# Layer 0 of a diffusion backbone: its six modulation units at every second step instead of at six steps in a row

## The chip, the core and the metric

The kernel runs on one core of one Trainium2 chip. The metric is the device time of one execution in microseconds (us). TensorE is written PE in the profile, VectorE DVE, ScalarE ACT, GpSimd POOL and SyncE SP.

## The reference, cut to what matters

Four layers work on 512 latent tokens x and 256 context tokens, each 1024 wide. Layers 0 and 3 are latent attention (MLA), layer 1 is windowed attention, layer 2 a long convolution. Ahead of each layer a vector of 3072 numbers is computed from the conditioning vector (cond @ w_mod: shift, scale and gate): shift and scale modulate the layer's input, and the gate scales its output.

```
for layer in range(DEPTH):
    mx = cond_x @ w_mod[layer] + b_mod[layer]
    mc = cond_c @ w_mod[layer] + b_mod[layer]
    shift_x, scale_x, gate_x = jnp.split(mx[:, None, :], 3, axis=-1)
    ...
    hx = rmsnorm(x, g_pre[layer]) * (1.0 + scale_x) + shift_x
    ...
    x = x + gate_x * rmsnorm(yx, g_post[layer])
def mla_mixer(hx, hc, w_in, g_q, w_q, g_kv, w_kv, w_out, with_ctx_out):
    cq_x, ckv_x, kr_x, gate_x = jnp.split(hx @ w_in, split_at, axis=-1)
    q_x = queries(cq_x, True)                  # rmsnorm(cq) @ w_q, rotary
    k_x, v_x = keys_values(ckv_x, kr_x, True)  # rmsnorm(ckv) @ w_kv
    ...
    y_x = (o_x.reshape(b, n, A_WIDTH) * jax.nn.silu(gate_x)) @ w_out
```

w_mod is 4 x 1024 x 3072 float32, that is 12 MB for a layer. It is read once and each number is used for two rows only, so its product costs TensorE little and the transfer queues much.

## The kernel before

The 768 tokens are six tiles of 128. Every matmul of weights with tokens is done as three products of a split pair (high and low part, lines 577 to 579 for a token tile, line 588 for a gate). The program is written tile by tile in Python, and a scheduler with its own timeline puts each engine's instructions in their final order; so moving a call moves instructions on all engines, later ones too.

**Two streams of weights.** Both take 512 KB chunks (4 KB in each of 128 partitions) through staging slots in the arena F, and all of their transfers are issued by SP from one queue in program order (line 211). A `Stream` issues the transfer of a chunk as soon as a slot is free and fewer than `cap_d` chunks wait. `W` carries the layers' own weights: a chunk is split into its high and low parts by ACT (line 230) and by DVE or POOL (line 233), and then its slot is free. `M` carries w_mod: a chunk is used as it comes by four matmuls of 256 columns (line 442), and its slot is free after them.

**A modulation unit** is 512 of the 3072 columns, four chunks, 16 matmuls L442 (the trace keeps two records for each, 32 in all). Units of kind "ab" (shift and scale of the next layer) then copy the result to the arena (ACT, line 455), turn it by four transposes (line 459) and add the bias (DVE). Units of kind "g" (the gate of this layer) copy it (line 480) and load a bias row (line 481). The copy of a unit lies in the arena F too, among the staging slots. `self.fill()` writes the next unit into the program. Layer 0 writes six: four "ab" of layer 1, and two "g" of layer 0; they are called unit 1 to unit 6 below.

**The steps of `layer_A` before attention** are 6 key tiles (`ps[:, 0:320]`, 24 matmuls of 320 columns each), 6 cq tiles (24 matmuls of 512 columns each), and 8 gates (24 matmuls of 512 and 24 of 256 columns each, weights ("gate", c) of 512 KB). The norm of a tile (`normed`) turns it by transposes too (line 721), and the rotary key is turned in line 761. Before the change a unit comes ahead of the key tiles 3, 4 and 5 and of the cq tiles 0, 1 and 2. From key tile 3 on, `M` may hold two chunks (`MC = 2`); after the gates one.

**The output of a layer** (`w_out_phase`): six token tiles, 48 matmuls L606 each, in two alternating pairs of PSUM banks (pb_69, pb_70). A tile is multiplied by the gate vector `g` and added to x by DVE (`post`, lines 566 and 567), which frees its banks for the next tile but one. `gates_out` (lines 483 to 499) makes `g` from the two "g" units: four matmuls (line 494) and four DVE products (line 495).

Layer 1's own modulation calls are in code that the change does not touch; they take chunks through the same streams.

Of the kernel before, what the change touches and what calls it, by code (L numbers as in the profile page):

```python
# [29 lines left out]
SU = 2  # L30
WX = {25: (3, 2), 27: (3, 2), 29: (3, 3)}
UKS = (3, 4)
UQ = 0
UC = 0
MC = 2
CH = ((0, 384),)
LS = 2
# [98 lines left out]
class Ring:  # L136
# [6 lines left out]
    def next(self):  # L143
        self.i += 1
        return self.blocks[self.i % len(self.blocks)]
# [125 lines left out]
class Kern:  # L271
# [430 lines left out]
    def layer_A(self, L, j, h, ctx_out, last):  # L702
# [9 lines left out]
        def normed(ps, n, dst, t):  # L712

            ssq = self.col()
            nc.scalar.activation(self.trash[:, 0:n], ps, AF.Square, accum_out=ssq)
            self.rstd(ssq, n)
            cn = self.fs(n)
            nc.vector.tensor_scalar(cn.ap, ps, ssq, None, op0=ALU.mult)
            pt = self.a()
            for k in range(n // P):  # L720
                nc.tensor.transpose(pt[:, P * k:P * k + P], cn.ap[:, P * k:P * k + P], self.ident)
            cn.free()
            self.split_ps(dst[:, 0, :, P * t:P * t + P], dst[:, 1, :, P * t:P * t + P],
                          pt[:, 0:n].rearrange("p (k n) -> p k n", n=P))

        UK = UKS[0 if ctx_out else 1]
        units = sum(f[:2] in (("ab", L + 1), ("g", L)) for f in self.fillers)

        wide = Banks(self.halves())
        ckv = self.rl(2 * 2 * T)  # L730
# [6 lines left out]
        self.W.pump(4, 3)  # L737
        wk = lambda k: (ws[k // 2][1][0][:, k % 2], ws[k // 2][1][1][:, k % 2])
        for t in order:
            if t == UK:  # L740
                self.M.cap_d = self.M.look_d = MC
            if units and t >= UK:
                self.fill()
                units -= 1
            ps = wide.next()
            self.mm_tok(ps[:, 0:320], h, t, wk, 320)
            normed(ps[:, 0:256], 256, ckvv, t)
            ks = small.next()
            kv4 = ks.v(2, 2, 64)
            if t < 4:  # L750
                kf = self.ropes.next()
                self.rope_ps(kf.v(1, 64), ps[:, 256:320].rearrange("p (a b) -> p a b", a=1), t, 1)
                src = kf.ap[:, 0:64]
            else:
                kf = None
                src = ps[:, 256:320]
            nc.scalar.activation(kv4[:, 0], src[:, None, :].to_broadcast([P, 2, 64]), AF.Copy)
            nc.vector.tensor_tensor(kv4[:, 1], src[:, None, :].to_broadcast([P, 2, 64]), kv4[:, 0].bitcast(F32), op=ALU.subtract)
            pt = self.a()
            for i in range(2):  # L760
                nc.tensor.transpose(pt[:, P * i:P * i + P], ks.ap[:, P * i:P * i + P].bitcast(F32), self.ident)
            nc.vector.tensor_copy(krv[:, :, P * t:P * t + P], pt[:, 0:256].rearrange("p (a b) -> p a b", a=2))
# [4 lines left out]
        cqv = cq.v(2, 4, TQ)  # L767
        ws = [self.W.take(("cq", k)) for k in range(0, KD, 2)]
        for t in (order if ctx_out else qt):
            if units and t >= UQ:  # L770
                self.fill()
                units -= 1
            ps = wide.next()
            self.mm_tok(ps, h, t, wk, 512)
            normed(ps, 512, cqv, t)
# [2 lines left out]

        spans = [(0, NX), (NX, NC)] if ctx_out else [(0, NX)]
        for c in range(8):  # L780
            if units and c >= UC:
                self.fill()
                units -= 1
            blk, (wh, wl) = self.W.take(("gate", c))
            outs = [self.a()[:, 0:n] for _, n in spans]
            self.mm_ch(outs, lambda part, k, i: self.h_at(h, part, k, *spans[i]), lambda k: (wh[:, k], wl[:, k]))
            blk.free()
            for (t0, n), o in zip(spans, outs):
                self.gate2(ogv[:, c, t0:t0 + n], o)
# [157 lines left out]
        units = [(hd, t) for hd in range(8) for t in qt]  # L947
# [891 lines left out]
```

## Time and profile before

| | us |
|---|---|
| median of 3 runs | 1942.29 (1940.02 to 1943.27) |
| the profiled execution, its own time | 1944.16 |
| its span in the trace | 1942.3 |
| TensorE busy in the span | 1817.6 |
| mean granted TensorE clock | 0.984 of full speed |

The span runs from the first to the last recorded instruction; 1.9 us of the profiled execution's time lie outside it. TensorE is busy for 94% of the span, so the time is that of TensorE's work and of the places where it waits.

### The profile page before, as it was taken

Reading aid. Unit: us, or ns where it says so; the run is one execution under the profiler, and the core shown is the slowest. Engines: PE = TensorE matmul, PEld = TensorE weight load, DVE = VectorE, ACT = ScalarE, POOL = GpSimd, SP = SyncE. Lnnn points to the kernel's source line nnn. Section 1 sums busy time; section 2 is a strip of 40 time slices with the busy share of each in tenths; the row PEclk is TensorE's granted clock in tenths of the full one; section 3 lists DMA queues with packets and bytes.
Section 4 is the critical chain, followed back from the end, with each engine's and each line's share of the span. In section 5 each row is a group of like instructions: output and inputs, shape, how many; then the busy total and the mean of one; then the engine's idle time right before and its main releaser. Section 6 shows DMA issues by size and latency. Waiting matters only on the chain. (4 is left out here: it accounts for less than half of the span.)

```text
span 1942.3 us, 30290 instructions
## 1 busy us (share of the span) xinstructions
PE 1817.6 (94%) x11628; PEld 1575.6 (81%) x11628; DVE 1172.8 (60%) x2365; ACT 813.3 (42%) x1688; POOL 520.7 (27%) x523
## 2 busy tenths in 40 slices
PE   5889899999999899999989999999989899999998
PEld 3567588999988888888858789999988687889986
DVE  6684234787755367777675456555665554477663
ACT  3463132554544255565654522222222353354451
POOL 5562000000223321222231344444443221000120
PEclk9899899999999999999999999999999899999999
DMA  7867521001133212222363622222222334410121
GB/s 217 251 178 228 163 77 33 22 23 45 44 109 109 66 54 78 77 74 68 100 216 108 201 80 69 76 76 77 77 66 65 106 123 142 108 34 23 44 66 65
DMA packets 186356, 186.31 MB, mean 96 GB/s; under 512 B 16600, under 2 KB 164952, under 8 KB 186212
## 3 DMA queue, kind: packets, MB, share of 16 engines
q1 hardware_dynamic: 186212, 184.39, 30.8%
q8 instruction: 91, 1.49, 0.3%
q14 instruction: 53, 0.43, 0.1%
HBM read 160.24 MB, written 24.12 MB: 95 GB/s over the span
## 5 line engine op out<-in xcount | busy, mean ns | idle before, releaser
L588 PE MATMUL pb<-arena_r 128*128 128x512 f32 (+1 forms) x1488 | 278.9, 341 | 1.6 <-ACT arena_r L555 1.2
L341 ACT ACTIVATE arena_r<-pa 128x384 fp32r<-128x384 f32 (+2 forms) x382 | 175.4, 479 | 205.4 <-PE pa L909 68.0
L588 PEld LDWEIGHTS pb<-arena_r 128*128 128x128 f32 x1488 | 228.4, 189 | 33.1 <-ACT arena_r L555 1.7
L342 DVE TENSOR_TENSOR arena_r<-pa,arena_r 128x384 fp32r<-128x384 f32 (+2 forms) x382 | 199.7, 537 | 86.7 <-ACT arena_r L341 84.7
L588 PE MATMUL pa<-arena_r,swing_R 128*128 128x512 f32 (+1 forms) x816 | 165.7, 355 | 0.6 <-DVE arena_r L342 0.4
L588 PEld LDWEIGHTS pa<-arena_r,swing_R 128*128 128x128 f32 x816 | 132.2, 188 | 21.9 <-DVE arena_r L342 0.6
L884 PE MATMUL pb<-arena_r 128*128 128x384 f32 (+1 forms) x720 | 141.4, 336 | 3.0 <-ACT arena_r L341 1.8
L606 PE MATMUL pb<-arena_r 128*128 128x512 f32 x552 | 135.5, 398 | 2.6 <-ACT arena_r L230 2.6
L233 POOL TENSOR_TENSOR swing_R<-arena_f,swing_R 128x1024 fp32r<-128x1024 f32 (+1 forms) x33 | 77.2, 2344 | 194.1 <-ACT swing_R L230 144.2
L606 PEld LDWEIGHTS pb<-arena_r 128*128 128x128 f32 x552 | 103.4, 190 | 26.0 <-ACT arena_r L230 2.9
L884 PEld LDWEIGHTS pb<-arena_r 128*128 128x128 f32 x720 | 118.9, 188 | 5.1 <-ACT arena_r L341 2.5
L679 POOL TENSOR_TENSOR arena_f<-arena_f 128x128 f32<-128x128 f32 (+1 forms) x44 | 21.0, 478 | 356.6 <-DVE small L892 180.2
L233 POOL TENSOR_TENSOR arena_r<-swing_F,arena_r 128x1024 fp32r<-128x1024 f32 x36 | 87.6, 2434 | 86.2 <-ACT arena_r L230 81.1
L358 POOL TENSOR_SCALAR small<-small 128x1 f32<-128x1 f32 x68 | 17.2, 253 | 345.7 <-ACT trash L564 145.8
L923 PE MATMUL pa<-arena_r 128*128 128x256 f32 x624 | 91.5, 286 | 2.1 <-DVE arena_r L342 2.1
L923 PEld LDWEIGHTS pa<-arena_r 128*128 128x128 f32 x624 | 81.8, 189 | 4.8 <-ACT arena_r L341 2.5
L1079 PE MATMUL pa<-swing_R,arena_r 128*128 128x256 f32 x576 | 78.8, 285 | 5.0 <-DVE arena_f L348 3.8
L442 PE MATMUL pa<-arena_f,cst 128*32 128x256 f32 x744 | 57.4, 410 | 24.8 <-DMA arena_f<-in_w_mod_dram 24.8
L888 DVE TENSOR_REDUCE small<-pb 128x1 f32<-128x768 f32 (+1 forms) x80 | 67.6, 847 | 21.5 <-PE pb L884 20.7
L230 ACT ACTIVATE arena_r<-swing_F 128x1024 fp32r<-128x1024 f32 x39 | 41.4, 1063 | 91.9 <-PE pb L588 55.9
L891 ACT ACTIVATE arena_f<-pb,small 128x768 f32<-128x768 f32 (+1 forms) x80 | 65.2, 817 | 32.8 <-DVE small L889 26.4
L1079 PEld LDWEIGHTS pa<-swing_R,arena_r 128*128 128x128 f32 x576 | 71.4, 189 | 7.3 <-DVE arena_f L348 5.2
(268 smaller groups left out, 4216.6 us busy)
## 6 DMA issues: line engine op xcount, KB each, us to landing
arena_f<-in_w_mod_dram SPq DMA_DIRECT2D x93, 512.0 KB
swing_F<-in_c_w_in_dram SPq DMA_DIRECT2D x31, 512.0 KB
kd<-arena_f SPq DMA_DIRECT2D x48, 256.0 KB
arena_f<-in_a_w_in_dram SPq DMA_DIRECT2D x24, 512.0 KB
arena_f<-kd SPq DMA_DIRECT2D x16, 768.0 KB
arena_f<-in_b_w_in_dram SPq DMA_DIRECT2D x20, 512.0 KB
x<-arena_f SPq DMA_DIRECT2D x18, 512.0 KB
arena_f<-in_a_w_out_dram SPq DMA_DIRECT2D x16, 512.0 KB
```

The costliest lines, as they stand in the source:

```text
L230: nc.scalar.activation(hi, view, AF.Copy)
L233: eng.tensor_tensor(lo, view, hi.bitcast(F32), op=ALU.subtract)
L341: self.nc.scalar.activation(hi, src, AF.Copy)
L342: self.nc.vector.tensor_tensor(lo, src, hi.bitcast(F32), op=ALU.subtract)
L442: nc.tensor.matmul(ps[32 * j:32 * j + 32, n0:n0 + 256], self.cst[:, 4 * kh + j, :], w[:, j, :], start=(kh == 0), stop=(kh == 1), skip_grou ...
L588: nc.tensor.matmul(out, l, rhs(part, k, i), start=(k == 0 and q == 0), stop=(k == kt - 1 and q == 2))
L606: nc.tensor.matmul(ys[:, 512 * hf:512 * hf + 512], ov[:, a, k - ks.start], wt[:, 0, 512 * hf:512 * hf + 512], start=(k == 0 and q == 0), s ...
L884: nc.tensor.matmul(S[:, 512 * b:512 * b + w], l, r[:, k0 + w * b:k0 + w * b + w], start=(q == 0), stop=(q == 4))
L888: nc.vector.tensor_reduce(mx, Sv, axis=AX.XY, op=ALU.max)
L891: nc.scalar.activation(pr.v(nb, w), Sv, AF.Exp, bias=mx, scale=sc, accum_out=sm)
L923: nc.tensor.matmul(o[:, 0:256], vv[:, a_, kt % 3, P * hh:P * hh + P], ptv[i // nh][:, b_, i % nh], start=(i == 0 and q == 0), stop=(i == n ...
L1079: nc.tensor.matmul(ps[:, 0:256], self.h_at(h, part, k, P * t, P), w, start=(k == 0 and i == 0), stop=(k == KD - 1 and i == 2))
```

## The change

A generator `modulate()` counts the steps: key tiles are steps 0 to 5, cq tiles 6 to 11, gates 12 to 19. In layer 0 it writes a unit at step 3 and at every second step from there: ahead of the key tiles 3 and 5, the cq tiles 1, 3 and 5, and of the second gate. In layer 3 the pitch is one and the first step is 4, as before.

```
-UQ = 0
-UC = 0
+UP = (2, 1)
...
-        UK = UKS[0 if ctx_out else 1]
         units = sum(f[:2] in (("ab", L + 1), ("g", L)) for f in self.fillers)
+
+        def modulate():
+
+            first, pitch = (UKS[0], UP[0]) if ctx_out else (UKS[1], UP[1])
+            for i in range(99):
+                if i == first:
+                    self.M.cap_d = self.M.look_d = MC
+                if i >= first and (i - first) // pitch < units and (i - first) % pitch == 0:
+                    self.fill()
+                yield
+
+        mods = modulate()
...
         for t in order:
-            if t == UK:
-                self.M.cap_d = self.M.look_d = MC
-            if units and t >= UK:
-                self.fill()
-                units -= 1
+            next(mods)
...
         for t in (order if ctx_out else qt):
-            if units and t >= UQ:
-                self.fill()
-                units -= 1
+            next(mods)
...
         for c in range(8):
-            if units and c >= UC:
-                self.fill()
-                units -= 1
+            next(mods)
```

The number of instructions of every kind on every engine stays what it was; their order changes. The lines after the constants move up by one (L442 becomes L441).

**First place: TensorE at unit 4.** Before, this is what stands in TensorE's order from the last chunk of unit 3 to the second cq tile. `pa_66<-arena_f,cst` is a chunk's matmuls, `pa_67<-ident,arena_f` the unit's transposes, `pb` a cq tile.

```order
L578 MATMUL pb_70<-swing_R,arena_r 128x512
L442 MATMUL pa_66<-arena_f,cst 32x256 x4
L579 MATMUL pb_70<-swing_R,arena_r 128x512
L577 MATMUL pb_70<-swing_R,arena_r 128x512
L578 MATMUL pb_70<-swing_R,arena_r 128x512
L579 MATMUL pb_70<-swing_R,arena_r 128x512
L459 MATMUL pa_67<-ident,arena_f 128x128 x4
L442 MATMUL pa_66<-arena_f,cst 32x256 x16
L721 MATMUL pa_68<-ident,arena_f 128x128 x4
L577 MATMUL pb_69<-arena_r 128x512
L578 MATMUL pb_69<-arena_r 128x512
```

After the change unit 4 begins between the third and the fourth cq tile, with one chunk alone (the second L441 row here; the first is unit 3's last chunk).

```order
L441 MATMUL pa_65<-arena_f,cst 32x256 x4
L577 MATMUL pb_69<-swing_R,arena_r 128x512
L578 MATMUL pb_69<-swing_R,arena_r 128x512
L576 MATMUL pb_69<-swing_R,arena_r 128x512
L577 MATMUL pb_69<-swing_R,arena_r 128x512
L578 MATMUL pb_69<-swing_R,arena_r 128x512
L576 MATMUL pb_69<-swing_R,arena_r 128x512
L577 MATMUL pb_69<-swing_R,arena_r 128x512
L578 MATMUL pb_69<-swing_R,arena_r 128x512
L458 MATMUL pa_66<-ident,arena_f 128x128 x4
L441 MATMUL pa_65<-arena_f,cst 32x256 x4
L720 MATMUL pa_67<-ident,arena_f 128x128 x4
```

The other three chunks of unit 4 follow one at a time. Its last one stands among the last matmuls of the fourth cq tile, and its transposes and the first chunk of unit 5 (the second L441 row here) behind them, ahead of the sixth cq tile:

```order
L576 MATMUL pb_69<-swing_R,arena_r 128x512
L441 MATMUL pa_65<-arena_f,cst 32x256 x4
L577 MATMUL pb_69<-swing_R,arena_r 128x512
L578 MATMUL pb_69<-swing_R,arena_r 128x512
L458 MATMUL pa_66<-ident,arena_f 128x128 x4
L720 MATMUL pa_67<-ident,arena_f 128x128 x4
L441 MATMUL pa_65<-arena_f,cst 32x256 x4
L720 MATMUL pa_68<-ident,arena_f 128x128 x4
```

Between unit 3's last chunk and unit 4's first there stood four matmuls of the cq tile, and now there are eight; unit 5's first chunk has two matmuls and eight transposes ahead of it. The sixteen L442 matmuls in a row are gone.

**Second place: SP's queue in layer 0**, from unit 3's last chunks on. `in_w_mod_dram` is a chunk of modulation, `in_a_w_in_dram 128x8x128` a gate's weights, `in_a_w_q_dram` the weights of the queries. Before:

```order
L211 DMA arena_f<-in_a_w_in_dram 128x8x128 x2
L211 DMA arena_f<-in_w_mod_dram 128x4x256 x2
L211 DMA arena_f<-in_a_w_in_dram 128x8x128 x2
L211 DMA arena_f<-in_w_mod_dram 128x4x256 x7
L481 DMA arena_f<-in_b_mod_dram 1x512
L211 DMA arena_f<-in_w_mod_dram 128x4x256 x2
L481 DMA arena_f<-in_b_mod_dram 1x512
L211 DMA arena_f<-in_a_w_in_dram 128x8x128 x3
L209 DMA arena_f<-in_a_w_q_dram 128x4x64 x4
```

After:

```order
L210 DMA arena_f<-in_a_w_in_dram 128x8x128 x3
L210 DMA arena_f<-in_w_mod_dram 128x4x256 x12
L210 DMA arena_f<-in_a_w_in_dram 128x8x128 x2
L210 DMA arena_f<-in_w_mod_dram 128x4x256
L480 DMA arena_f<-in_b_mod_dram 1x512
L208 DMA arena_f<-in_a_w_q_dram 128x4x64 x3
L210 DMA arena_f<-in_w_mod_dram 128x4x256
L208 DMA arena_f<-in_a_w_q_dram 128x4x64
L210 DMA arena_f<-in_w_mod_dram 128x4x256
L210 DMA arena_f<-in_a_w_in_dram 128x8x128 x3
```

Ahead of the first row here SP issues thirteen of the 24 chunks before, and nine after. Before, four gates come close together, with two chunks between them; after, three gates come first, then twelve chunks without a gate, and the last three chunks are strung out among gates and query weights.

**Third place: TensorE at layer 1's output**, where the change moves instructions though its own lines do not run there. Before, this is the first token tile (pb_70) and the beginning of the second (pb_69), with the last four matmuls of attention (L1188); every chunk of the two "g" units (L442) stands ahead of these rows:

```order
L1188 MATMUL pa_67<-arena_r 128x256 x2
L606 MATMUL pb_70<-swing_R,arena_r 128x512 x14
L606 MATMUL pb_70<-arena_r 128x512 x2
L1188 MATMUL pa_67<-arena_r 128x256 x2
L606 MATMUL pb_70<-arena_r 128x512 x16
L494 MATMUL pa_66<-arena_f,sel 128x512
L606 MATMUL pb_69<-swing_R,arena_r 128x512 x4
L606 MATMUL pb_70<-arena_r 128x512 x4
L494 MATMUL pa_65<-arena_f,sel 128x512
L606 MATMUL pb_70<-arena_r 128x512 x8
L494 MATMUL pa_67<-arena_f,sel 128x512
L606 MATMUL pb_69<-swing_R,arena_r 128x512 x14
```

After, from the end of the first token tile to the first matmuls of the third, which uses pb_70 again (L605 was L606, L493 was L494):

```order
L441 MATMUL pa_65<-arena_f,cst 32x256 x12
L605 MATMUL pb_70<-arena_r 128x512 x8
L493 MATMUL pa_68<-arena_f,sel 128x512
L493 MATMUL pa_66<-arena_f,sel 128x512
L605 MATMUL pb_69<-swing_R,arena_r 128x512 x14
L441 MATMUL pa_65<-arena_f,cst 32x256 x4
L605 MATMUL pb_69<-arena_r 128x512 x30
L493 MATMUL pa_65<-arena_f,sel 128x512
L493 MATMUL pa_67<-arena_f,sel 128x512
L605 MATMUL pb_70<-swing_R,arena_r 128x512 x18
```

Five chunks, 20 matmuls L441, have gone from the end of attention into the first two tiles of the output (one of the five, a group of four, stands a few rows ahead of these). The last two matmuls of `gates_out` now stand right ahead of the third tile; before, they stood within the first. On DVE the four products L494 (L495 before), then L565 and L566 of the first tile follow each other in this order. Further up, in layer 1's attention, each of the first six units stands in three groups of chunks, where it stood in two.

## Rows read from the trace of the kernel before

**Rows 1.** The page: busy time of the engines in the span.

```profile
PE 1817.6 (94%) x11628; PEld 1575.6 (81%) x11628; DVE 1172.8 (60%) x2365; ACT 813.3 (42%) x1688; POOL 520.7 (27%) x523
```

**Rows 2.** Windows of 10 us: busy PE, PEld, DVE, ACT, POOL; clock; DMA share; GB/s.

```profile
190.00:200.00 10.00, 9.27 (x68) 6.25 (x67) 3.12 (x7) 3.32 (x8) 1.49 (x4) 1.00 0.87 261
200.00:210.00 10.00, 2.30 (x22) 1.07 (x24) 1.72 (x4) 1.11 (x2) 0.00 (x0) 0.67 0.76 212
210.00:220.00 10.00, 10.00 (x66) 6.54 (x62) 1.97 (x5) 1.20 (x2) 0.00 (x0) 0.81 0.50 160
220.00:230.00 10.00, 8.59 (x61) 5.50 (x53) 1.45 (x2) 2.57 (x6) 1.49 (x4) 1.00 0.63 208
230.00:240.00 10.00, 9.53 (x62) 6.63 (x59) 1.44 (x2) 2.05 (x5) 0.11 (x1) 1.00 0.17 53
```

**Rows 3.** What PE waits for, 150 to 300 us: total, times, longest.

```profile
PE pa L442 <- DMA arena_f<-in_w_mod_dram: 8.7, 3, 6.8
```

**Rows 4.** Timeline of PE about units 3 and 4: start, duration, idle before and releaser.

```profile
192.75 0.64 PE L442 MATMUL pa<-arena_f,cst 128*32 128x256 f32 x8 [0.73 <-DMA arena_f<-in_w_mod_dram]
...
198.53 0.64 PE L442 MATMUL pa<-arena_f,cst 128*32 128x256 f32 x8
...
199.44 0.40 PE L577 MATMUL pb<-swing_R,arena_r 128*128 128x512 f32 x1
...
201.17 0.66 PE L459 MATMUL pa<-ident,arena_f 128*128 128x128 f32 x4 [0.86 <-ACT arena_f L455]
208.66 3.64 PE L442 MATMUL pa<-arena_f,cst 128*32 128x256 f32 x32 [6.84 <-DMA arena_f<-in_w_mod_dram]
212.23 1.12 PE L721 MATMUL pa<-ident,arena_f 128*128 128x128 f32 x4
213.00 0.78 PE L577 MATMUL pb<-arena_r 128*128 128x512 f32 x1
```

**Rows 5.** The same timeline about units 5 and 6.

```profile
218.05 0.60 PE L459 MATMUL pa<-ident,arena_f 128*128 128x128 f32 x4
218.58 0.64 PE L442 MATMUL pa<-arena_f,cst 128*32 128x256 f32 x8
...
222.20 1.07 PE L442 MATMUL pa<-arena_f,cst 128*32 128x256 f32 x16 [1.10 <-DMA arena_f<-in_w_mod_dram]
223.59 0.66 PE L721 MATMUL pa<-ident,arena_f 128*128 128x128 f32 x4 [0.31 <-DVE arena_f L718]
224.00 0.47 PE L577 MATMUL pb<-arena_r 128*128 128x512 f32 x1
...
232.05 0.66 PE L721 MATMUL pa<-ident,arena_f 128*128 128x128 f32 x4 [0.47 <-DVE arena_f L718]
```

**Rows 6.** Issues on SP's queue in that stretch: start, duration of the issue.

```profile
188.83 0.37 SPq L211 DMA_DIRECT2D arena_f<-in_w_mod_dram  x1
...
199.91 0.37 SPq L211 DMA_DIRECT2D arena_f<-in_w_mod_dram  x1
200.37 0.46 SPq L211 DMA_DIRECT2D arena_f<-in_a_w_in_dram  x1
201.91 0.37 SPq L211 DMA_DIRECT2D arena_f<-in_a_w_in_dram  x1
202.38 1.18 SPq L211 DMA_DIRECT2D arena_f<-in_w_mod_dram  x1
...
218.72 0.37 SPq L211 DMA_DIRECT2D arena_f<-in_w_mod_dram  x1
```

**Rows 7.** Timeline of PE at layer 1's output.

```profile
994.90 1.50 PE L442 MATMUL pa<-arena_f,cst 128*32 128x256 f32 x24
996.34 0.51 PE L1188 MATMUL pa<-arena_r 128*128 128x256 f32 x2
...
1025.42 6.97 PE L606 MATMUL pb<-arena_r 128*128 128x512 f32 x30
1032.23 1.80 PE L606 MATMUL pb<-swing_R,arena_r 128*128 128x512 f32 x7
```

**Rows 8.** What PE waits for, 980 to 1040 us, and a window as in rows 2.

```profile
PE pa L442 <- DMA arena_f<-in_w_mod_dram: 2.2, 3, 1.4
...
980.00:1000.00 20.00, 16.14 (x133) 11.14 (x131) 17.53 (x43) 13.50 (x37) 9.38 (x8) 0.91 0.64 199
```

**Rows 9.** Timeline of DVE at layer 1's output.

```profile
1022.37 0.69 DVE L495 TENSOR_TENSOR arena_f<-pa,arena_f 128x512 f32<-128x512 f32 x1 [1.99 <-PE pa L494]
1022.97 1.22 DVE L566 TENSOR_TENSOR pb<-pb,arena_f 128x1024 f32<-128x1024 f32 x1
1024.11 1.22 DVE L601 TENSOR_TENSOR arena_r<-arena_f,arena_r 128x1024 fp32r<-128x1024 f32 x1
1025.24 1.28 DVE L567 SCALAR_TENSOR_TENSOR arena_f<-pb,small,arena_f 128x1024 f32<-128x1024 f32 x1
```

## The prediction, made before the changed kernel was run

> **What bounds the kernel now.** I read the page's busy times first: TensorE works for 94% of the span [rows 1]. A change that adds and removes no instruction can only win what TensorE idles or runs slowly, so I looked for the stretch in which it does. In the windows of layer 0 one stands out. From 200 to 210 us TensorE is busy for 2.30 of 10 us, while the windows about it show 8.6 to 10; its granted clock there is 0.67, and 0.81 in the next window [rows 2]. The waits say for what: modulation chunks, three times, 8.7 us in total, 6.8 the longest [rows 3].
>
> The timeline shows where. Unit 4 is sixteen L442 matmuls in a row, right behind unit 3. Its first chunk begins at 208.66 after 6.84 us without work [rows 4]. SP's queue says why: that chunk was issued only at 202.38, since the slot that it needed held the copy of unit 3, which the transposes of 201.17 read last. Three more transfers of 512 KB, at 199.91, 200.37 and 201.91, were issued just ahead [rows 4, 6]. So it took 6.3 us to come, and a chunk that is issued with an emptier queue comes sooner: 3.9 us from 188.83 to its use at 192.75, and 3.5 us from 218.72 to 222.20 [rows 4 to 6]. I take 3.7.
>
> **What can come back in layer 0.** The idle times of TensorE around units 3 to 6 are 0.73, 0.86 and 6.84 [rows 4] and 1.10, 0.31 and 0.47 [rows 5], in all 10.3 us. The clock adds to it. Three chunks in a row take 1.44 us at full clock (994.90 to 996.34), 0.48 each [rows 7]; unit 4's four took 3.57 instead of 1.92. The four transposes behind took 0.77 (212.23 to 213.00), against 0.41 elsewhere (223.59 to 224.00) [rows 4, 5]. That is 2.0 us lost to the lower clock, and 12.3 us is the most that layer 0 can give back.
>
> **What remains there.** A 512-column matmul takes 0.227 us (30 of them from 1025.42 to 1032.23) [rows 7], and four transposes 0.53 (218.05 to 218.58) [rows 5]. By the order after the change, two chunks are still late.
> Unit 4's first chunk now has eight matmuls and four transposes ahead of it, 8 x 0.227 + 0.53 = 2.35 us, from when its slot comes free. Against 3.7 us of transfer that leaves a wait of 1.4.
> Unit 5's first chunk has less: two matmuls, four unit transposes, four norm transposes. The transposes of a unit came about 2.1 us behind its last chunk (199.1 to 201.17) because of ACT's copy, of which 0.86 was idle time over four matmuls [rows 4]. With two matmuls 1.5 of it is idle. Then 0.53 + 0.41 of transposes end at 3.0, and the chunk comes at 3.7: 0.7 more, 2.2 us in all.
> The other chunks have 20 or more matmuls ahead, 4.5 us or more, and I take their waits as gone. The two short waits for DVE (0.31 and 0.47) stay, 0.8. So 4.4 us remain. Bounds: nothing remains, if the queue is empty enough; or each of the two waits grows to the 6.84 that was seen, which would make it about 14 and eat the gain.
> Chunks that stand alone cost more than chunks in a row: from 198.53 to 199.44 a single chunk and one matmul take 0.91, that is 0.68 for the chunk [rows 4], 0.20 over the 0.48. The change makes fifteen groups of twelve: 0.6 us.
> Layer 0 gives 12.3 - 4.4 - 0.6 = 7.3 us.
>
> The Trainium skill, "DMA: Bandwidth & Descriptors", section "Anatomy of one DMA — SWDGE (gpsimd) path", states about 2 us plus the bytes at 436 GB/s for a transfer on another path than SP's; worked out from it, an estimate, 512 KB would come in 3.2 us, the two waits would shrink by 0.5 each, and the gain would be 1.0 larger; the trace's 3.5 and 3.9 decide.
>
> SP's queue takes the gates' weights past the chunks now. That costs nothing: a gate is 24 x 0.227 + 24 matmuls of half the columns, about 8 us, so a set of weights that comes two gates ahead has 16 us of cover against a transfer of 3.7. From 230 to 240 us the queue is almost empty (DMA share 0.17) [rows 2], so the chunks that move there meet little. Without that cover each late gate would cost up to its transfer, 3.7.
>
> **What it moves in layer 1.** Five chunks go from the end of attention into the output tiles, where TensorE works without a gap. There they cost their whole time: two alone at 0.68, three in a row at 3 x 0.48 + 0.20, together 3.0. At the end of attention three waits for chunks fall away, 2.2 us [rows 8]. Of the chunks' own time there, between 0 and 3.0 comes back: TensorE is busy for 16.1 of 20 us in that stretch, and DVE for 17.5 [rows 8]. I take the middle, 1.5.
> The last two matmuls of `gates_out` now stand right ahead of the third output tile, which needs the banks of the first. These come free only after DVE has made two products of `g`, multiplied the tile and added it: 0.60 + 0.60 + 1.14 + 1.28 = 3.6 us by the starts and the last duration [rows 9]. Before, the last of this chain ended at 1026.5 and the third tile began at 1032.23 [rows 7, 9], so it was hidden behind 5.7 us of the second tile. Now its cover is gone but for the second of the two matmuls, 0.2: 3.4 us of waiting.
> The split of layer 1's six units into three groups instead of two costs up to 6 x 0.20 = 1.2, down to 0 where TensorE waits for DVE anyway; I take 0.6.
> Layer 1 loses 3.0 + 3.4 + 0.6 - 2.2 - 1.5 = 3.3 us. Layer 3 has the same steps as before; what the scheduler shuffles elsewhere I put at 0, within 2 us either way.
>
> **The sum** is 3.3 - 7.3 = -4.0. The profiled span of 1942.3 becomes 1938.3, and with the 1.9 us outside it the profiled execution 1940.2. That execution was 1.9 above the median of the runs, so the median goes from 1942.3 to **1938.3 us**, 0.2% less. 0.2%, 3.9 us, is also about what a measurement of this kernel tells from no change; the likeliest case lies right on it.
>
> **The rivals.**
> *Full return:* layer 1 gives nothing back on balance, since the end of attention shortens by all of the chunks' time and the third tile's wait is shorter than its chain. For it: TensorE's part of attention has no other large wait there than those 2.2 us. Against it: the 3.4 us chain is in the order. Time: 1942.3 - 7.3 = 1935.0; with no wait left in layer 0 either, 1930.6.
> *The clock falls at each new wait:* one wait of 6.84 us becomes waits of 1.4 and 2.2, and 3.4 in layer 1. If each costs the 2.0 us of clock that the long one cost, the time is 1938.3 + 6.0 = 1944.3, no change that can be told. Against it: after 1.10 us without work at 222.20 the window shows a clock of 1.00 [rows 2, 5]. For it: the 3.4 lies between that and 6.84, and no row decides it.
> The Trainium skill, "TensorE: Matmul & The Clock Gate", section "HAM oscillation — how this bites in real kernels", describes a kernel whose waits for transfers between short stretches of matmuls throw the clock down again at every one; by that rule this change trades one fall for three, and the rows of 222.20 speak against it for the shortest waits.
> *Slower:* the chunks that moved into layer 1's output tiles come late there, where nothing covers them and the weights of the next layer and the tokens share the queue. A wait as long as the worst of layer 0, 6.84, with its 2.0 of clock gives 1938.3 + 8.8 = 1947.1. It decides from waits of 5.9 us there: 4.0 to use up the gain and 3.9 for the bound, less the clock's 2.0. Against it: 22 matmuls or more stand between issue and use of these chunks, 5 us against 3.7.
>
> **How the numbers follow.** The likeliest case gets 0.48, and as it lies on the bound, 0.25 of it counts as faster and 0.23 as the same. Full return gets 0.25, the clock 0.16, slower 0.11. So faster is 0.50, same 0.39, slower 0.11. The range runs from 1932, between the two times of full return, to 1945, which holds the clock's 1944.3 and leaves the slower case out. The likeliest case alone has 1935.5 to 1941.
>
> **What would show it.** In the windows of layer 0 no 10 us have less than 8 us of work, and the clock stays at 1.00. The waits for chunks there fall from 8.7 to about 3, in two places, and the waits for ACT's copy rise to about 1.5. Behind layer 1's second output tile a wait for DVE (L566) of 3 to 4 us appears. Wrong would be: a wait over 5 us on a chunk anywhere in layer 0, no wait ahead of the third tile, or a difference that comes from layers 2 and 3.

## The result

The changed kernel is slower: 1954.3 us median (1952.07 to 1957.01, 4 runs) against 1942.78 us (1940.02 to 1945.15, 4 runs) on the same chip, a ratio of 1.0069 with a 95% interval of 1.0051 to 1.0087. The prediction was 1938.3 us. The profiled execution's span is 1952.7 us, 10.4 more than before, and TensorE's busy share is one point lower.

Layer 0 did about what was forecast. The windows of the changed kernel, with the columns of [rows 2], have no 10 us with less than 8 us of work:

```profile
200.00:210.00 10.00, 8.55 (x68) 5.56 (x59) 2.72 (x6) 2.57 (x6) 1.48 (x4) 1.00 0.45 130
210.00:220.00 10.00, 10.00 (x56) 7.16 (x55) 0.69 (x1) 0.61 (x2) 0.00 (x0) 1.00 0.25 81
220.00:230.00 10.00, 8.31 (x44) 5.43 (x43) 3.40 (x8) 4.22 (x8) 1.48 (x4) 0.83 0.69 210
```

TensorE's waits from 150 to 300 us name chunks for 2.6 us where it was 8.7 [rows 3]:

```profile
PE pa L441 <- DMA arena_f<-in_w_mod_dram: 2.6, 2, 1.6
```

TensorE's timeline shows the two:

```profile
206.08 0.42 PE L441 MATMUL pa<-arena_f,cst 128*32 128x256 f32 x4 [1.03 <-DMA arena_f<-in_w_mod_dram]
...
224.66 0.64 PE L441 MATMUL pa<-arena_f,cst 128*32 128x256 f32 x8 [1.57 <-DMA arena_f<-in_w_mod_dram]
```

The 6.84 us wait at unit 4 [rows 4] has become 1.03 and 1.57. But the time came back, and more, in layer 1, which the diff does not touch. Three lines of the program mark its course, each with the first and the last start of its matmuls: the first scores of layer 0 (L884 before, L886 after), the value product of layer 1's attention (L1188, L1190), and the first transposes of layer 2 (L1545, L1547). Before:

```profile
L884 PE MATMUL pb<-arena_r x720: 278/334/446, 340.2 to 1878.5; 128*128 128x384 f32 x160, 128*128 128x256 f32 x20
...
L1188 PE MATMUL pa<-arena_r x352: 274/282/415, 694.7 to 1012.1; 128*128 128x256 f32 x176
...
L1545 PE MATMUL pa<-ident,swing_F x96: 270/272/328, 1118.7 to 1506.6; 128*128 128x128 f32 x96
```

After:

```profile
L886 PE MATMUL pb<-arena_r x720: 277/334/446, 331.9 to 1888.8; 128*128 128x384 f32 x160, 128*128 128x256 f32 x20
...
L1190 PE MATMUL pa<-arena_r x352: 274/282/580, 689.7 to 1014.9; 128*128 128x256 f32 x176
...
L1547 PE MATMUL pa<-ident,swing_F x96: 270/272/331, 1130.7 to 1516.2; 128*128 128x128 f32 x96
```

Layer 0's scores begin 8.3 us earlier. Layer 1's first value product is only 5.0 earlier. The attention from there to its last one takes 325.2 us instead of 317.4, and from there to layer 2's first transposes it is 115.8 instead of 106.6. So layer 1 loses 17.0 us between its first value product and layer 2, and layer 2 begins 12.0 us late.

The wait that was forecast ahead of the third output tile is there, by TensorE's timeline:

```profile
1037.10 1.88 PE L493 MATMUL pa<-arena_f,sel 128*128 128x512 f32 x4
1042.99 1.22 PE L605 MATMUL pb<-swing_R,arena_r 128*128 128x512 f32 x2 [4.02 <-DVE arena_f L566]
```

and by that of DVE, with the chain in front of it (the products of `g`, L565 and L566):

```profile
1039.14 1.28 DVE L494 TENSOR_TENSOR arena_f<-pa,arena_f 128x512 f32<-128x512 f32 x2
1040.34 1.22 DVE L565 TENSOR_TENSOR pb<-pb,arena_f 128x1024 f32<-128x1024 f32 x1
1041.66 1.28 DVE L566 SCALAR_TENSOR_TENSOR arena_f<-pb,small,arena_f 128x1024 f32<-128x1024 f32 x1
```

Four microseconds of 17 are thus seen as one wait. The stretch from the first value product to layer 2 shows what the rest is made of, with the columns of [rows 2]; before, then after:

```profile
694.70:1118.70 424.00, 399.76 (x2885) 339.40 (x2884) 279.84 (x668) 236.62 (x572) 110.64 (x127) 1.00 0.35 112
```

```profile
689.70:1130.70 441.00, 410.13 (x2886) 344.59 (x2884) 281.00 (x668) 236.63 (x572) 111.44 (x127) 0.98 0.34 109
```

TensorE does the same work there and is busy for 10.4 us longer; it is idle for 6.6 us longer, the 4.02 among them. A good part of the busy time is the granted clock. In windows of 20 us from 690 to 1070 us it is below 1.00 in one window before:

```profile
970.00:990.00 20.00, 14.98 (x106) 10.87 (x106) 18.51 (x35) 14.09 (x31) 13.51 (x8) 0.91 0.69 230
```

and in three after, these two and the one from 1030 to 1050 us (0.83, shown at the end):

```profile
930.00:950.00 20.00, 18.93 (x147) 16.55 (x148) 13.63 (x34) 10.75 (x30) 2.26 (x5) 0.91 0.30 93
...
990.00:1010.00 20.00, 16.59 (x107) 13.57 (x108) 16.24 (x41) 14.18 (x38) 8.94 (x7) 0.74 0.46 143
```

Busy time times the missing share of the clock, an estimate from these windows, is 1.3 us before and 8.7 us after (1.7, 4.3 and 2.7). So of the 17.0 us about 7.4 are the lower clock and 6.6 are waiting; the other 3 us of busy time are not placed. The split is rough, since the ends of matmuls in the profile are modelled.

What these losses have in common shows in no row of waits, but in the addresses that the two programs give to their buffers. Arena F has 13760 words in each partition. Staging slots lie on a grid of 1024 words, counted down from 12736. At layer 1's start the program lays the attention's rings (three of 656 words, two of 256) into the first gaps from 6144 upwards. One chunk of layer 1's own weights, fetched during layer 0's output, still waits in a slot then; which slot it got depends on which slot came free longest ago. Printed from the allocation of both programs:

```
before   chunk waits at 8640   rings at 6144, 6800, 7456, 8112, 8368 (to 8624)
         staging slots left for layer 1: 11712, 10688, 9664, 8640
after    chunk waits at 7616   rings at 6144, 6800, 8640, 9296, 9552 (to 9808)
         staging slots left for layer 1: 11712, 10688, 7616
```

In the changed program the third ring does not fit between 7456 and the chunk at 7616. It goes above it, into slot 8640, and the last ring reaches into slot 9664. Layer 1's two streams and the copies of its units then have three slots instead of four. In the last of the attention's eight blocks, once the buffers of the rotary step are freed, it is four instead of five.

### The profile page after: what moved, and what is told of

Same layout as the page of the kernel before. It is cut to its first block, busy times and chain, and to the rows that moved or that the text cites. A ratio compares the mean times of both kernels' runs of the same rounds, so it can differ in the third digit from the quotient of the medians.

```text
span 1952.7 us, 30291 instructions
## 1 busy us (share of the span) xinstructions
PE 1823.9 (93%) x11628; PEld 1577.4 (81%) x11628; DVE 1173.2 (60%) x2365; ACT 812.5 (42%) x1688; POOL 519.0 (27%) x523
## 5 line engine op out<-in xcount | busy, mean ns | idle before, releaser
L886 PE MATMUL pb<-arena_r 128*128 128x384 f32 (+1 forms) x720 | 141.5, 337 | 3.0 <-ACT arena_r L340 1.8
L605 PE MATMUL pb<-arena_r 128*128 128x512 f32 x552 | 134.1, 394 | 2.2 <-ACT arena_r L229 2.0
L605 PEld LDWEIGHTS pb<-arena_r 128*128 128x128 f32 x552 | 102.1, 188 | 26.1 <-issue 2.4
L886 PEld LDWEIGHTS pb<-arena_r 128*128 128x128 f32 x720 | 119.0, 188 | 5.2 <-ACT arena_r L340 2.5
L605 PE MATMUL pb<-swing_R,arena_r 128*128 128x512 f32 x288 | 75.8, 412 | 4.0 <-DVE arena_f L566 4.0
```

Source lines behind the costliest of these rows:

```text
L605: nc.tensor.matmul(ys[:, 512 * hf:512 * hf + 512], ov[:, a, k - ks.start], wt[:, 0, 512 * hf:512 * hf + 512], start=(k == 0 and q == 0), s ...
L886: nc.tensor.matmul(S[:, 512 * b:512 * b + w], l, r[:, k0 + w * b:k0 + w * b + w], start=(q == 0), stop=(q == 4))
```

## The experiments

**Theory A:** layer 1 lost its time to the missing slot. **Theory B:** it lost it because units at every second step leave its streams in another phase, or by a chance order of instructions, wherever the rings lie. The first four kernels were run together (the kernel before: 1941.97 us median there), then four (1940.63), then two (1942.15).

**e1_chunk_above.** The changed kernel, with a lower bound on the slots in the pump of layer 0's output (`nxt == 1`), and the bound's test in `Arena.slot`:

```
+                if si == 0 and o * GRAN < self.low:
+                    continue
                 if (st[o:o + n] < self.BUSY).all():
...
+                    self.F.low = 8640 if nxt == 1 else 0
                     self.W.pump(self.W.cap_w + 1, self.W.cap_w)
+                    self.F.low = 0
```

> The changed kernel, but the four weight chunks of layer 1 that are fetched during layer 0's output may only take staging slots from offset 8640 of the arena F upwards, so that the rings of layer 1 lie where they lay before the change and layer 1's attention has four staging slots again instead of three. Theory A (layer 1 lost its time because a fetched chunk at offset 7616 pushed a ring into a fourth staging slot): layer 1 costs what it cost before, the wait for DVE ahead of the third output tile is gone, and what layer 0 saved stays: 1936 to 1941 us. Theory B (layer 1 lost its time because units at every second step come later and leave its streams in another phase, wherever the rings lie): within 3 us of the changed kernel, 1951 to 1957 us.

Measured: 1936.8 us, ratio 0.9973 (0.9961 to 0.9985). Theory A's time, and faster than before, though 8.0 us are lost where layer 1 starts (9.5 us ahead at layer 0's scores, 1.5 at layer 1's first value product; see e7).

**e2_slot_held.** The kernel before, with one slot held from the rings' allocation to the end of layer 1's attention:

```
         sums = Ring(self, "fl", 256, SU)
+        hold = self.F._grab(0, 9664 // GRAN, 1024 // GRAN, 1024)
...
         for r in (small, pts, prob, sums):
             r.free()
+        hold.free()
```

> The kernel before, with one thing done: in layer 1's attention one staging slot of 1024 words (offset 9664 of the arena F) is held and not used, so that three are left of four. Layer 0 is unchanged. Theory A (the count of staging slots in layer 1): slower by what the changed kernel lost in layer 1, 12 to 20 us: 1954 to 1962 us, units of layer 1 in three groups of chunks, and a wait for DVE of 3 to 4 us ahead of the third output tile. Theory B (not the slots, but the moved units): 1941 to 1945 us.

Measured: 1960.87 us, ratio 1.0100 (1.0085 to 1.0116), 18.9 us more. Its rows for the value product and layer 2's first transposes:

```profile
L1189 PE MATMUL pa<-arena_r x352: 274/282/583, 694.2 to 1025.3; 128*128 128x256 f32 x176
...
L1547 PE MATMUL pa<-ident,swing_F x96: 270/272/476, 1144.0 to 1524.6; 128*128 128x128 f32 x96
```

TensorE's waits from 990 to 1100 us have the one ahead of the third tile:

```profile
PE pb L606 <- DVE arena_f L567: 4.0, 1, 4.0
```

Layer 1's value product begins where it began before (694.2 against 694.7), and from there to layer 2 it takes 449.8 us, against 424.0. The units come in three groups (mostly 2, 1 and 1 chunks), as in the changed kernel; in the kernel before they mostly come as 3 and 1. Nothing was moved in layer 0; the slot alone does it, the 4.0 us wait and the three groups included.

**e3_from_step_2** and **e4_from_step_4.** The changed kernel with `UKS = (2, 4)` and `UKS = (4, 4)`, so the first unit comes one step earlier or later. Both leave four slots.

> The changed kernel with the first unit one step earlier: every second step from the third key tile (step 2) to the first gate. By the allocation this leaves the fetched chunk at offset 8640 and four staging slots in layer 1. Theory A: 1936 to 1941 us, as with the chunk moved. Theory B: units at every second step lose in layer 1 as in the changed kernel, 1950 to 1957 us.

> The changed kernel with the first unit one step later: every second step from the fifth key tile (step 4) to the third gate. By the allocation this too leaves four staging slots in layer 1. Theory A: 1936 to 1942 us. Theory B: as late as or later than in the changed kernel, 1950 to 1958 us.

Measured: 1948.03 us, ratio 1.0037 (1.0021 to 1.0053), and 1943.53 us, ratio 1.0007 (0.9992 to 1.0021). Both theories missed. Layer 1 is right by A: from its first value product to layer 2's transposes it takes 423.6 and 425.6 us. But layer 0 gains nothing there: its scores begin at 340.6 and 340.5 us. Their waits for chunks from 150 to 300 us, e3 and then e4:

```profile
PE pa L441 <- DMA arena_f<-in_w_mod_dram: 8.7, 5, 2.5
```

```profile
PE pa L441 <- DMA arena_f<-in_w_mod_dram: 10.0, 5, 3.7
```

So the spacing by itself is not what helps layer 0: one long wait has become five shorter ones of about the same sum. Begun at step 3, as in the change, two are left. The median of e3 is 3 us above its profiled execution (1944.88), and where that lies one profile does not show.

**e5_slot_barred.** The changed kernel with one slot barred instead of a bound: `self.F.bar = 7616 if nxt == 1 else -1` in the same two places, tested as `o * GRAN == self.bar`.

> The changed kernel, with one staging slot (offset 7616 of arena F) barred for layer 1's first weight chunks while layer 0's output runs. Unlike e1_chunk_above, which allowed only slots from 8640 upwards, the chunks may use all others. The last chunk then lies at 5568, the rings of layer 1 at 0 to 2480, and four slots are left. Theory A (slots left in layer 1): layer 1 costs what it cost before, 1932 to 1938 us, without the 7.6 us that e1_chunk_above lost where layer 1 starts. Theory B (e1_chunk_above was fast by a chance order of instructions and not by the slots): 1945 to 1957 us.

Measured: **1932.58 us**, ratio 0.9959 (0.9945 to 0.9972), the fastest here and faster than both kernels.

```profile
L893 PE MATMUL pb<-arena_r x720: 277/334/446, 332.3 to 1870.5; 128*128 128x384 f32 x160, 128*128 128x256 f32 x20
...
L1197 PE MATMUL pa<-arena_r x352: 274/283/415, 686.1 to 1002.7; 128*128 128x256 f32 x176
...
L1554 PE MATMUL pa<-ident,swing_F x96: 270/272/328, 1110.1 to 1492.4; 128*128 128x128 f32 x96
```

Layer 0 is 7.9 us ahead of before at its scores, and 8.6 us are still there at layer 1's value product and at layer 2: layer 1 takes 424.0 us, to the tenth what it took before. The wait for DVE is gone.

**e6_one_chunk.** The changed kernel, with the bound only for the one chunk that waits: `k.F.low = 8640 if key == ("v", 1) else 0` ahead of its fetch.

> The changed kernel, where of layer 1's first weight chunks only the one that still waits at its start (the second half of the value weights) is kept to slots from offset 8640 upwards. It then lies at 12736, the rings lie where they lay before, four slots are left. Theory A: 1932 to 1938 us. Theory B: 1945 to 1957 us.

Measured: 1949.39 us, ratio 1.0041 (1.0029 to 1.0053). A missed here, and three rows at layer 1's start say why:

```profile
620.88 2.34 POOL L237 TENSOR_TENSOR swing_R<-arena_f,swing_R 128x1024 fp32r<-128x1024 f32 x1 [8.37 <-ACT swing_R L234]
...
623.25 0.42 DVE L681 TENSOR_TENSOR arena_f<-pb,rope 128x256 f32<-128x256 f32 x1 [5.00 <-POOL swing_R L237]
...
624.06 0.58 PE L581 MATMUL pb<-swing_R,arena_r 128*128 128x256 f32 x1 [9.62 <-DVE arena_f L682]
```

With four slots the rest of layer 1 takes 424.5 us, as A has it. But the start waits 9.62 us for the rotary step on DVE (L681 and L682), and that waits until POOL has split a weight chunk. Printed from the allocation, the buffers of the rotary step lie at 8640 in this program, in the slot of that chunk; in the changed kernel they lie at 12736, and the first rotary step stands at 615.69 us instead of 623.25. To keep one chunk from a slot has moved another buffer.

**e7_before_confined.** The kernel before with the edit of e1_chunk_above alone.

> The kernel before with the edit of e1_chunk_above alone: layer 1's first weight chunks may only take slots from 8640 upwards. Units at six steps in a row. Four slots are left in layer 1 with and without it. If that edit is no gain by itself, the late first chunks cost 3 to 8 us where layer 1 starts: 1943 to 1950 us, and the gain of e1_chunk_above is that of the moved units. If the edit is what made e1_chunk_above fast, it is at 1935 to 1939 us here too.

Measured: 1948.42 us, ratio 1.0046 (1.0032 to 1.0059). The bound costs the start of layer 1 dearly, three waits of TensorE from 600 to 660 us:

```profile
PE pb L580 <- DVE arena_f L570: 4.6, 1, 4.6
PE pb L580 <- ACT swing_R L233: 2.0, 1, 2.0
PE pb L581 <- POOL swing_R L236: 1.9, 1, 1.9
```

So the edit is no gain by itself, and e1's gain is that of the moved units with four slots.

**e8_third_step.** `UP = (3, 1)`, a unit at every third step. By the allocation the chunk is at 7616 again, with three slots.

> The changed kernel with a unit at every third step instead of every second (steps 3 to 18). By the allocation the fetched chunk lies at 7616 as in the changed kernel and three slots are left in layer 1. Theory A: layer 1 loses 12 to 20 us again, the wait for DVE ahead of the third output tile is there; 1950 to 1962 us. Theory B (the phase of the units decides): as the two other starts showed, anywhere from 1942 to 1950 us.

Measured: 1956.02 us, ratio 1.0076 (1.0061 to 1.0091). Layer 1 takes 445.0 us, and the 4.0 us wait is there. A called it from the allocation alone.

**e9_held_early** and **e10_held_late** hold the slot in the kernel before for a part of the attention only, up to its last block of eight, or in that block alone: in the first, `hold.free()` stands where the ropes, the buffers of the rotary step, are freed (`if c == 7`); in the second another slot, the one at 12736 that the ropes leave, is taken there, so that the last block has four slots instead of five.

> The kernel before with the slot of e2_slot_held held only until the last of layer 1's eight blocks of attention begins, where the ropes are freed and the streams may take more. If the cost of the three slots is paid where they are missing, the attention up to there costs its 8 to 13 us more, and the output of layer 1 is as before, without the 4 us wait ahead of its third tile: 1950 to 1955 us. If the late chunks carry over to the output, about all of it is there: 1957 to 1962 us.

> The kernel before with one staging slot held only in the last of the eight blocks of layer 1's attention. If the cost in the output comes from this last block, the output loses 8 to 12 us with the 4 us wait ahead of the third tile, and the attention before it nothing: 1950 to 1955 us. If the chunks are late because of what happened earlier, nothing changes: 1941 to 1945 us.

Measured: 1960.46 us, ratio 1.0087 (1.0062 to 1.0113), and 1955.98 us, ratio 1.0069 (1.0050 to 1.0089). The same two rows of e9_held_early, then of e10_held_late:

```profile
L1189 PE MATMUL pa<-arena_r x352: 274/282/582, 694.2 to 1027.8; 128*128 128x256 f32 x176
...
L1547 PE MATMUL pa<-ident,swing_F x96: 270/272/327, 1134.6 to 1523.5; 128*128 128x128 f32 x96
```

```profile
L1188 PE MATMUL pa<-arena_r x352: 274/282/415, 692.5 to 1007.4; 128*128 128x256 f32 x176
...
L1547 PE MATMUL pa<-ident,swing_F x96: 270/272/328, 1127.7 to 1514.9; 128*128 128x128 f32 x96
```

Held early, the attention takes 333.6 us (317.4 before) and the output 106.8 (106.6). Held late, the attention takes 314.9 and the output 120.3, and the 4.0 us wait for L567 is there as in e2. Each cost is paid where the slot is missing, and neither carries over. Both costs were expected smaller: the attention of e9 lost 16.2 us, where 8 to 13 were expected and e2 lost 13.7, and the output of e10 lost 13.7, where 8 to 12 were expected. By its total e9 fell into the range of the other answer, and only its profile, of an execution 3.3 us above the median, tells the two apart; another 4 us came behind layer 1. e10 lies 1 us above its range.

All twelve profiles by slots in layer 1 (up to the last block), from its first value product to layer 2's first transposes, from the rows of those two lines:

| slots | kernels | us |
|---|---|---|
| four | before; e1, e3, e4, e5, e6, e7 | 424.0; 423.3, 423.6, 425.6, 424.0, 424.5, 425.4 |
| three | after; e2, e8 | 441.0; 449.8, 445.0 |
| one missing for a part | e9, e10 | 440.4, 435.2 |

## Why the prediction was wrong

**Layer 0: right.** It forecast 7.3 us. In the five programs with six units in a row layer 0's scores begin at 337.6 to 340.2 us (mean 339.0), and in the four with the change's spacing and start at 330.7 to 332.3 (mean 331.6): 7.4 us. The mechanism holds too: from 150 us to the scores TensorE idles 5.7 us less (9.0 for 14.7), where 10.3 - 4.4 = 5.9 was forecast. The sum is closer than its terms. The single waits came out smaller, 1.03 and 1.57 in place of 1.4 and 2.2, and no wait for ACT's copy is named from 150 to 300 us, where one of 1.5 was forecast. Against that the clock of the window 220 to 230 is 0.83, where the forecast had 1.00.

**Layer 1's output: the wait right, its cause missed.** The forecast had 3.4 us ahead of the third tile and five chunks in the output at 3.0. The wait is 4.02, and the chunks are there. The whole output lost 9.2 us; the wait, the 3.0 and the clock of the window 1030 to 1050 (2.7 by the estimate above) make 9.7. But e5, with the same units in layer 0, has no such wait. The order that makes it was a consequence of the missing slot (e10), not of the units' new steps.

**Layer 1's attention: the step that failed.** By the forecast's terms the attention should have become 3.1 us shorter: 2.2 and 1.5 came back, and 0.6 was lost. It became 7.8 us longer, although five chunks had left it. The 0.6 is the term that failed. The text noticed that "the split of layer 1's six units into three groups instead of two costs up to 6 x 0.20 = 1.2", priced the extra groups, and did not ask why a unit in untouched code should come in three. They are a sign of the missing slot (e2), and e9 shows that the slot alone costs the attention 16.2 us in the kernel before. In the changed kernel the attention's busy time grew by 4.1 us and its idle time by 3.7. The sum had no term for a lower clock there.

**Elsewhere.** "What the scheduler shuffles elsewhere I put at 0, within 2 us either way": between layer 0's scores and layer 1's first value product the changed kernel lost 3.3 us (8.3 ahead, then 5.0); in e5 it lost nothing. The windows place most of it at layer 1's start: 620 to 640 us have a clock of 0.91 and 660 to 670 of 0.83, 2.8 us by the same estimate, where the kernel before and e5 have 1.00 throughout. What brought the clock down there is not traced. From layer 2's start to the end it got 1.6 us back.

**The rivals.** The slower one had the right place for half of the loss, the output of layer 1, and the wrong mechanism: no chunk was late there by a row of the trace, since from 980 to 1050 us none of TensorE's waits is for a chunk. The clock's rival came near in size and only in part in place. It put 6.0 us on three new waits, and the waits of 1.57 and 4.02 do lie in windows with a clock of 0.83 (220 to 230, 1030 to 1050 us). But the estimate for layer 1 alone is 7.4 us, and most of it lies in the attention, beside waits that were not forecast. The sum of full return, 7.3 us less than before, is about what e5 reached (8.05 less), once the slot was given back.

What stays open is how, step by step, the missing slot costs the attention its time. TensorE's waits for chunks in the attention are not longer than in e5; first the changed kernel, then e5:

```profile
PE pa L441 <- DMA arena_f<-in_w_mod_dram: 5.3, 8, 1.4
```

```profile
PE pa L444 <- DMA arena_f<-in_w_mod_dram: 5.7, 9, 0.9
```

What the traces do show is that layer 1's own weights are fetched later. These are the first chunk of modulation that SP issues behind layer 1's first value product and the next chunk of weights, in the kernel before:

```profile
702.22 0.37 SPq L211 DMA_DIRECT2D arena_f<-in_w_mod_dram  x1
...
723.39 0.46 SPq L211 DMA_DIRECT2D arena_f<-in_b_w_in_dram  x1
```

and the same two in the changed kernel:

```profile
697.30 0.37 SPq L210 DMA_DIRECT2D arena_f<-in_w_mod_dram  x1
...
725.61 0.37 SPq L210 DMA_DIRECT2D arena_f<-in_b_w_in_dram  x1
```

The weights leave 21.2 us behind the modulation before, and 28.3 after. In e5, with four slots, it is 21.2 again, and in e2, e8 and e9, with three, 28.4 to 28.9. TensorE's added idle time is spread over short waits for DVE and ACT, and the lower clock lies among them. That weights which come later upset the order of the work, and so bring these waits, is argued from this, not shown.

## What to carry to other kernels

A change to the order of work changes the order in which buffers come free, and a first-fit allocator turns that into another layout far behind the change. Before the time of such an edit is forecast, the addresses should be compared as well as the instructions, above all the number of staging slots in each stage; here that was one line of the allocation, and it decided 17 to 26 us. When untouched code shows another grouping of its transfers, the cause is worth finding before the groups are priced.

The same instructions can be busy for longer: here 410.1 us instead of 399.8. When a stage grows, the granted clock is worth reading beside the waits; an estimated 7.4 of the 17.0 us went there.

A long wait that is spread out is not gone by that: with the same spacing, begun one step earlier or later, five waits add up to the same 8.7 to 10.0 us.

## What the runs showed of the hardware

TensorE's granted clock fell beside waits that were shorter than the forecast expected. In the changed kernel the longest wait from 220 to 230 us is 1.57 us, and the clock of that window is 0.83; in the kernel before a wait of 1.10 us left it at 1.00 [rows 2, 5]. The 4.02 us ahead of the third output tile of layer 1 lie in this window of the changed kernel:

```profile
1030.00:1050.00 20.00, 15.98 (x61) 11.86 (x55) 8.02 (x8) 5.07 (x8) 2.01 (x6) 0.83 0.33 121
```

In the changed kernel's attention the clock fell beside several short waits. From 985 to 990 us TensorE is busy for half of the time, from 990 to 1000 its clock is at half speed, and no wait from 980 to 1010 us is longer than 2.54 us:

```profile
985.00:990.00 5.00, 2.49 (x22) 1.43 (x20) 2.12 (x6) 2.95 (x6) 2.81 (x2) 1.00 0.88 285
990.00:995.00 5.00, 4.37 (x20) 4.27 (x20) 3.79 (x9) 3.61 (x11) 2.38 (x1) 0.50 0.66 185
995.00:1000.00 5.00, 4.50 (x21) 3.84 (x20) 3.98 (x10) 4.11 (x9) 3.65 (x3) 0.50 0.21 68
```
